# A streaming encoder step on one core: the first block's loads re-timed, the forget chain cut in three, one scaling moved to ScalarE

## The chip, the core and the metric

The kernel runs on one core of a Trainium2 chip. TensorE (PE in the profile) multiplies matrices; PEld is its loading of the stationary operand. VectorE (DVE), ScalarE (ACT) and GpSimd (POOL) do elementwise work. SyncE (SP) issues nearly all DMAs. Each engine works through its own instructions in order, and waits on semaphores for the others and for DMAs. The metric is the device time of one execution, in microseconds (us).

## The reference

One layer of a hybrid encoder takes 2048 prompt frames and 64 sample frames that have a cache of 512 earlier ones. All is float32 with D = 1024.

```python
h = rmsnorm(x, g_pre)
fq, fk, fv, ff, fg, dq, dk, dv, dg = split(h @ w_in)          # widths 512, ff 8
logf = log_sigmoid(ff + b_f);  cum = cumsum(logf)             # over cache and new frames
# fox: 8 heads of 64, causal
s = fq.fk / 8 + cum[q] - cum[k];  fox_o = softmax(s) @ fv
# diff: 4 heads, two halves of 64, chunk-causal, T5 bias by relative position
lam = exp(sum(lq1*lk1)) - exp(sum(lq2*lk2)) + 0.2
p = softmax(q1.k1/8 + bias) - lam * softmax(q2.k2/8 + bias);  diff_o = p @ dv
diff_o = rmsnorm(diff_o, subln_g) * 0.8
mixed = concat(fox_o * silu(fg), diff_o * silu(dg))
y = x + rmsnorm(mixed @ w_out, g_post)
```

The results are y for prompt and sample, and the new rows of fk, fv, logf, dk and dv.

## The kernel before

Matrices are multiplied in split form: each operand is a rounded part (h) and a remainder (l), and three products hh, hl, lh are summed in PSUM. So each weight tile that is loaded is cast on ScalarE (`wh`, L776) and subtracted on VectorE or GpSimd (`wl`, L777).

**Blocks.** The prompt is cut into four blocks of 512 frames (tiles of 128 frames; the sample is a fifth tile, number 16, of block 0). `Proj.block(b)` projects one block, group by group: in blocks 0 and 2 the order is fv, fg, fk, fq, dg, dk, dq, dv, in blocks 1 and 3 the reverse. A group takes eight weight tiles of 128x512, one for each 128 rows. `nat` makes one frame tile of a natural group (8 steps of three matmuls, then an evacuation `nat_out` that scales by the row's 1/rms, `rs`); `qgroup` makes q transposed. The loop counts groups with `gi`. Block 0 is different: its weights go through staging tiles `wst` in the pool "pp" (8 tiles, two weight tiles in each), its first group (`nat_first`) multiplies all five frame tiles step by step into five PSUM buffers, and the first two tiles of its second group use the PSUM tag "pt" (three buffers), which they share with `ptq`, the sums of squares of x that VectorE reads into `xv` (L1123), and with the forget logits' accumulators. In its first four groups block 0 rotates its accumulators over five PSUM buffers (`acc`).

**Side work.** `stats(b+1)` squares the next block's x: loads `xn` (L1072), squares with a sum on ScalarE (L1084), then a short column step and a row step. Its pieces are appended one by one after frame tiles of groups 2 to 5. `forget(b)` makes the eight forget logits, and returns functions that come later: `columns` (log-sigmoid on small tiles, L1163 to L1188, on ScalarE and VectorE in turn), `sums` (cumulative sum to DRAM, `CUM`) and in block 0 `sample` (the same for the cache: loads `crev` (L1212), scans it (L1216), writes `csum`). `prologue2` loads subln, the lambda vectors `lamt` (L1415), relT and cbias, computes lambda, and builds the line of relative biases on GpSimd.

**Attention.** `Attn` runs about one block behind, interleaved with the next projection. It asks for keys (`kg`, pool "kk"), values, q, biases (`bias` and `strip`, pool "bb", two tiles) and gates (pool "gg", two tiles) ahead of use, in rings. `diff` makes the scores of both halves; exponentials `prob` are up to 2048 keys wide in two tiles of 1024. `combine` scales the second softmax by a per-row factor `cc` and adds it to the first: for keys up to 1024 in one VectorE instruction (L596), beyond that by a scaling (L593) and an addition (L594), both on GpSimd. `Out` multiplies by w_out beside the last block's attention and at the end.

**Order.** Every piece of work is a function with an estimated cost. They are put on one list, `line`, with a place in time in estimated TensorE microseconds; `put` spreads a list over an interval, and single entries have a fixed place (prologue 20, prologue2 110). The list is sorted and called, and the framework's list scheduler then orders each engine's instructions, moving work ahead when, by its own estimate, its inputs and a buffer of its pool are there. A pool with n buffers under a tag makes the n+1st tile wait until the first one is released. The pool "ef" has four tiles of 128x512, tag "er" two.

Of the kernel before, what the change touches and what calls it, by code (L numbers as in the profile page):

```python
# [91 lines left out]
def hybrid_step(ctx: ExitStack, tc: tile.TileContext, ins, outs):  # L92
# [68 lines left out]
    class Attn:  # L161
# [393 lines left out]
        def diff(self, u, pair, ctxu, last, sample=False):  # L555
# [9 lines left out]
            for j, t in enumerate(tiles):  # L565
# [14 lines left out]
                def combine(j=j, n=n):  # L580
                    if j == 0:
                        e["c"] = sm.tile([P, 2], F32, name="ci", tag="ci")
                    st = sts[j]
                    c = sm.tile([P, 2], F32, name="cc", tag="cc")
                    st[0]["total"]()
                    st[1]["total"]()
                    nc.vector.reciprocal(out=c[:rows, 0:1], in_=st[1]["s"][:rows, 0:1])
                    nc.vector.scalar_tensor_tensor(out=c[:rows, 1:2], in0=st[0]["s"][:rows, 0:1], scalar=neglam[:rows],
                                                   in1=c[:rows, 0:1], op0=ALU.mult, op1=ALU.mult)
                    for h, c0 in enumerate(range(0, n, 2 * BLK)):  # L590
                        p0, p1 = (x["P"][h][:rows, :min(n - c0, 2 * BLK)] for x in st)
                        if h:
                            nc.gpsimd.tensor_scalar(out=p1, in0=p1, scalar1=c[:rows, 1:2], scalar2=None, op0=ALU.mult)  # L593
                            nc.gpsimd.tensor_tensor(out=p0, in0=p0, in1=p1, op=ALU.add)  # L594
                        else:
                            nc.vector.scalar_tensor_tensor(out=p0, in0=p1, scalar=c[:rows, 1:2], in1=p0, op0=ALU.mult,  # L596
                                                           op1=ALU.add)
                    nc.vector.reciprocal(out=e["c"][:rows, j:j + 1], in_=st[0]["s"][:rows, 0:1])
# [124 lines left out]
    class Proj:  # L723
# [72 lines left out]
        def block(self, b):  # L796
# [27 lines left out]
            for gi, g in enumerate(order):  # L824
# [10 lines left out]
                else:  # L835
# [3 lines left out]
                    for tt in ts:  # L839
                        last = tt[-1] == tl[-1]  # L840
                        th += self.nat(b, g, tt, w, x, cols, st, last and ends, last and lastg)
                        if 2 <= gi <= 5:
                            th += sq[:1]
                            sq = sq[1:]
                        if b == 0 and gi == 1 and tt[0] == tl[2]:
                            th += row0
                        if gi == 1 and tt[0] == tl[0]:
                            th += [(0.1, fn) for fn in after[:1]]
                            after = after[1:]
                        elif gi == 1 and tt[0] == tl[1 if b else 2]:  # L850
                            th += [(0.1, fn) for fn in after]
                            after = []
                if b and gi == 0:
# [153 lines left out]
        def qgroup(self, b, g, w, x, nt, st, freew):  # L1007
# [4 lines left out]
            for c in range(4):  # L1012
                e = {}
                for i, segs in enumerate(pieces):
# [22 lines left out]
                    def evac(c=c, i=i, e=e, segs=segs, t0=t0, N=N):  # L1037
                        f = self.p["e"].tile([P, BLK], F32, name="qf", tag="ef")
                        hl = self.p["raw"].tile([P, BLK], F32R, name="qhl", tag="raw") if nt > BLK and not i else \
                            self.p["e"].tile([P, 2 * BLK], F32R, name="qhl", tag="er", bufs=2)  # L1040
                        nc.vector.tensor_tensor(out=f[:, :N], in0=e[i][:, :N], in1=st["rbc"][:, t0:t0 + N],
# [15 lines left out]
        def stats(self, b, st):  # L1057
# [4 lines left out]

            todo = [(i, t, hf) for i, t in enumerate(tl) for hf in (0, 1)]


            lead = 2 if b == 1 else 1

            def load(n):
                i, t, hf = todo[n]
                e[n] = self.p["raw"].tile([P, BLK], F32, name="xn", tag="raw") if b == 1 else \  # L1070
                    self.p["e"].tile([P, BLK], F32, name="xn", tag="ef")
                nc.sync.dma_start(out=e[n], in_=xp[t * P:(t + 1) * P, hf * BLK:(hf + 1) * BLK])  # L1072

            def square(n):
                def go():
                    i, t, hf = todo[n]
                    if not n:
                        e["ss"] = sm.tile([P, 2, 8], F32, name="xss", tag="xss", bufs=2)
                        nc.vector.memset(e["ss"], 1.0)
                        for m in range(lead):  # L1080
                            load(m)
# [47 lines left out]
        def forget(self, b, x, nt, st):  # L1129
# [5 lines left out]
            def alloc():  # L1135
                e["z"] = self.p["raw"].tile([P, BLK + DEC], F32, name="z8", tag="z", bufs=1)
            th.append((0.0, alloc))
            for c0, N in ((0, BLK), (BLK, DEC))[:1 + (b == 0)]:
# [17 lines left out]
            def columns():  # L1156
# [19 lines left out]
                nc.scalar.activation(out=a, in_=a, func=AF.Exp, scale=-1.0)  # L1176
                d, lw, m = e["fd"], e["fl"], e["fm"]
                nc.vector.tensor_scalar(out=d, in0=a, scalar1=1.0, scalar2=None, op0=ALU.add)
                nc.scalar.activation(out=lw, in_=d, func=AF.Ln)
                nc.vector.tensor_scalar(out=d, in0=d, scalar1=-1.0, scalar2=None, op0=ALU.add)  # L1180
# [22 lines left out]
            def sample():  # L1203
# [4 lines left out]
                nc.tensor.transpose(pt[:8, :DEC], z[:DEC, 32:40], ident[:DEC, :DEC])  # L1208
                c = self.p["e"].tile([P, BLK], F32, name="csum", tag="ef")[:8]
                c2 = sm.tile([8, DEC], F32, name="csn", tag="csn", bufs=1)  # L1210
                r = self.p["e"].tile([P, BLK], F32, name="crev", tag="ef")[:8]
                nc.sync.dma_start(out=r, in_=clf)  # L1212
                nc.vector.tensor_tensor_scan(out=c2, data0=ones[:8].to_broadcast([8, DEC]), data1=pt[:8, :DEC],
# [188 lines left out]
    def prologue(e):  # L1402
# [6 lines left out]
        nc.sync.dma_start(out=fb, in_=bass.AP(fbias.tensor, fbias.offset, [[0, P], [1, 8]]))  # L1409

    def prologue2(e):
        nc.sync.dma_start(out=subl, in_=subln)

        lam = e.tile([P, BLK], F32, name="lamt", tag="ef")
        nc.sync.dma_start(out=lam[:, :256], in_=bcast_row(lams, 256))  # L1415
        ee = sm.tile([P, 4], F32, name="lame", tag="lame", bufs=1)
        for i in (0, 1):
            nc.vector.tensor_tensor_reduce(out=lam[:, 256:320], in0=lam[:, 128 * i:128 * i + 64],
                                           in1=lam[:, 128 * i + 64:128 * i + 128], scale=1.0, scalar=0.0,
# [4 lines left out]

        rt = sm.tile([4, 32], F32, name="relT", tag="relT", bufs=1)
        nc.sync.dma_start(out=rt, in_=relT)
        nc.sync.dma_start(out=cbias, in_=bass.AP(relT.tensor, relT.offset + 15, [[0, P], [32, 4]]))
        nc.vector.tensor_scalar(out=cbias, in0=cbias, scalar1=-1.0, scalar2=None, op0=ALU.mult)
# [134 lines left out]
```

## Time and profile before

| | us |
|---|---|
| median of 3 runs | 1772.97 (1772.33 to 1780.28) |
| profiled execution | 1778.38 |
| its span in the profile | 1776.6 |
| TensorE busy | 1715.1 (97%) |
| weight loads busy | 1462.7 (82%) |
| VectorE busy | 1208.8 (68%) |
| ScalarE busy | 1127.0 (63%) |
| GpSimd busy | 761.7 (43%) |

The span is the time between the first and the last recorded instruction. A row of waits reads: who waited, for whom, total us, how often, the longest. A row of a timeline reads: start, length, engine, line, operation, output<-inputs, shape, count, and in square brackets how long the engine was idle before it and what ended that. A row of a window gives each engine's busy time and instruction count, the granted TensorE clock (1.00 is full speed), the mean busy share of the 16 DMA engines and GB/s.

### The profile page before, as it was taken

The numbers are of one execution on the slowest core, as the hardware profiler recorded it, in microseconds if no ns is written. First come the engines' busy times: TensorE is split into PE (matmuls) and PEld (weight loads), VectorE is DVE, ScalarE is ACT, GpSimd is POOL, SyncE is SP. The second block draws the span as 40 slices with busy tenths as digits, with TensorE's granted clock in tenths as the row PEclk, the third lists the DMA queues.
The fourth block names the chain that finished last, engine by engine and source line by source line (L and its number), as shares of the span: only waits on it lengthen the run. The fifth ranks groups of instructions, "written<-read, shape, count | busy, mean of one in ns | idle before, by whom it ended". The sixth has DMA issues, their size and how long they took to land.

```text
span 1776.6 us, 31312 instructions
## 1 busy us (share of the span) xinstructions
PE 1715.1 (97%) x9844; PEld 1462.7 (82%) x9844; DVE 1208.8 (68%) x3289; ACT 1127.0 (63%) x2518; POOL 761.7 (43%) x1075
## 2 busy tenths in 40 slices
PE   8899999999999999999999999999989999999998
PEld 6697988888787877888888888888878888888887
DVE  5424565566786666766777687877788787767674
ACT  5636465586676765675676567667676656666663
POOL 2313135364444533443324235645685655323341
PEclk9899999999999999999999999999999999999999
DMA  9785688889767667877677666767674455355433
GB/s 249 229 218 185 201 279 284 242 268 278 210 224 242 209 184 222 260 206 243 213 249 212 208 178 196 225 201 224 204 235 155 158 184 180 129 204 166 155 109 111
DMA packets 278981, 369.94 MB, mean 208 GB/s; under 512 B 32080, under 2 KB 167404, under 8 KB 278816
## 3 DMA queue, kind: packets, MB, share of 16 engines
q1 hardware_dynamic: 278000, 365.57, 67.0%
q0 software_dynamic: 672, 2.38, 0.5%
q8 instruction: 78, 1.28, 0.3%
q14 instruction: 87, 0.71, 0.1%
q10 hardware_dynamic: 144, 0.00, 0.0%
HBM read 263.87 MB, written 106.35 MB: 208 GB/s over the span
## 4 chain that ended last, share of the span: by engine, by line
PE 71%; DMA 11%; DVE 6%; ACT 4%; issue 3%; POOL 3%; SPq 1%; DVEq 0%; POOLq 0%; ACTq 0%
PE S L348 11%; PE pt L487 8%; PE acc L871 8%; PE acc L872 7%; PE acc L873 7%; PE av L518 6%; PE avd L518 4%; PE acc L1026 3%; PE acc L1027 3%; PE acc L1028 3%; DMA wraw<-in_w_in 3%; PE acco L1325 2%; PE acco L1327 2%; PE acco L1326 2%; ACT prob L369 2%
## 5 line engine op out<-in xcount | busy, mean ns | idle before, releaser
L369 ACT ACTIVATE prob<-prob,mn 128x1024 f32<-128x1024 f32 (+8 forms) x400 | 356.6, 893 | 152.8 <-DVE mn L356 151.6
L348 PE MATMUL S<-kg,qg 128*128 128x512 f32 (+4 forms) x1344 | 370.7, 371 | 10.9 <-DVE mn L356 6.1
L494 DVE TENSOR_TENSOR ptl<-pt,pth 128x512 fp32r<-128x512 f32 (+3 forms) x456 | 283.6, 637 | 80.1 <-ACT pth L493 77.7
L871 PE MATMUL acc<-wh,xx 128*128 128x512 f32 x752 | 300.6, 403 | 14.3 <-DVE xv L1123 6.2
L872 PE MATMUL acc<-wl,xx 128*128 128x512 f32 x752 | 299.5, 400 | 3.9 <-DVE wl L777 3.9
L873 PE MATMUL acc<-wh,xx 128*128 128x512 f32 x752 | 298.6, 398 | 0.3 <-DVE xx L745 0.2
L493 ACT CAST pth<-pt 128x512 fp32r<-128x512 f32 (+3 forms) x456 | 238.1, 546 | 91.1 <-PE pt L487 78.4
L487 PE MATMUL pt<-ident,prob 128*128 128x128 f32 (+2 forms) x1692 | 256.4, 273 | 7.7 <-DVE prob L596 5.2
L348 PEld LDWEIGHTS S<-kg,qg 128*128 128x128 f32 (+1 forms) x1344 | 225.5, 187 | 46.4 <-DVE mn L356 11.5
L487 PEld LDWEIGHTS pt<-ident,prob 128*128 128x128 f32 (+2 forms) x1692 | 199.3, 141 | 28.1 <-DVE prob L596 6.1
L777 POOL TENSOR_TENSOR wl<-wraw,wh 128x512 fp32r<-128x512 f32 x126 | 169.7, 1363 | 90.9 <-ACT wh L776 85.0
L871 PEld LDWEIGHTS acc<-wh,xx 128*128 128x128 f32 x752 | 143.4, 191 | 43.8 <-issue 6.6
L872 PEld LDWEIGHTS acc<-wl,xx 128*128 128x128 f32 x752 | 143.4, 191 | 30.0 <-DVE wl L777 4.6
L873 PEld LDWEIGHTS acc<-wh,xx 128*128 128x128 f32 x752 | 143.0, 190 | 28.6 <-DVE xx L745 1.2
L518 PE MATMUL av<-pth,vg 128*128 128x256 f32 (+1 forms) x576 | 157.5, 292 | 3.9 <-ACT pth L493 2.3
L405 POOL TENSOR_TENSOR dg<-bias,cmask 128x128 f32<-128x128 f32 (+1 forms) x136 | 65.2, 479 | 208.6 <-DVE mn L356 134.0
L450 POOL TENSOR_SCALAR gate<-gate,rr 128x64 f32<-128x64 f32 (+1 forms) x136 | 64.2, 482 | 182.8 <-DMA gate<-GS 98.9
L518 PE MATMUL av<-ptl,vg 128*64 128x256 f32 (+1 forms) x576 | 138.2, 281 | 1.5 <-DVE ptl L494 1.5
L776 ACT CAST wh<-wraw 128x512 fp32r<-128x512 f32 x168 | 100.6, 621 | 58.3 <-DMA wraw<-in_w_in 44.1
L518 PE MATMUL avd<-pth,vg 128*128 128x256 f32 (+1 forms) x576 | 131.4, 287 | 0.4 <-ACT pth L493 0.4
L356 DVE CUSTOM_DVE_ANT_0 prob<-S,bias,mn 128x512 f32<-128x512 f32 (+4 forms) x200 | 115.4, 577 | 13.6 <-PE S L348 6.6
L518 PEld LDWEIGHTS av<-pth,vg 128*128 128x128 f32 x576 | 109.5, 191 | 14.2 <-ACT pth L493 2.7
(261 smaller groups left out, 3604.6 us busy)
## 6 DMA issues: line engine op xcount, KB each, us to landing
wraw<-in_w_in SPq DMA_DIRECT2D x168, 256.0 KB, 5.2
vg<-VS SPq DMA_DIRECT2D x80, 512.0 KB, 6.3
qg<-QD SPq DMA_DIRECT2D x128, 256.0 KB, 4.4
kg<-KS SPq DMA_DIRECT2D x64, 512.0 KB, 5.1
wst<-in_w_in SPq DMA_DIRECT2D x64, 256.0 KB, 6.3
out<-ef SPq DMA_DIRECT2D x64, 256.0 KB, 2.6
VS<-vhl SPq DMA_DIRECT2D x32, 512.0 KB, 4.8
KS<-khl SPq DMA_DIRECT2D x32, 512.0 KB, 4.4
```

The lines of the kernel that those rows point to most:

```text
L348: nc.tensor.matmul(S[:rows, :c1 - c0], q()[s][:, qc:qc + rows], kg()[ki][:, c0 - k0:c1 - k0], start=(s == 0), stop=(s == 1))
L356: nc.vector.tensor_tensor_reduce(out=pr[:rows, a - p0:b - p0], in0=S[:rows, a - c0:b - c0], in1=ap()[:rows, a - b0:b - b0], scale=1.0, sca ...
L369: nc.scalar.activation(out=pr, in_=pr, func=AF.Exp, scale=-1.0, bias=st["m"][:rows, i - 1:i], accum_out=st["s"][:rows, h:h + 1])
L487: nc.tensor.transpose(pt[:rk, off:off + rows], self.key_tile(sts[j], rows, kt, rk), ident[:rows, :rows])
L493: nc.scalar.copy(h[:rk, :off], pt[:rk, :off])
L494: nc.vector.tensor_tensor(out=l[:rk, :off], in0=pt[:rk, :off], in1=r32(h[:rk, :off]), op=ALU.subtract)
L518: nc.tensor.matmul(st["av"][:vs.stop - vs.start, j0 * rows:W], ctxu["v"][kt // 4][:rk, kt % 4, vs], g["p"][part][:rk, o:o + w], start=(kt ...
L776: nc.scalar.copy(h, raw[:, :BLK])
L777: (nc.vector if many or k % 4 == 3 else nc.gpsimd).tensor_tensor(out=l, in0=raw[:, :BLK], in1=r32(h), op=ALU.subtract)
L871: nc.tensor.matmul(a, x[0][:, c0:c0 + rows], wh, start=s, stop=False)
L872: nc.tensor.matmul(a, x[0][:, c0:c0 + rows], wl, start=False, stop=False)
L873: nc.tensor.matmul(a, x[1][:, c0:c0 + rows], wh, start=False, stop=e)
```

## The change

Six edits:

1. `stats`: the pieces are appended in block 0 after tiles of groups 4 and 5 only, and block 1's x is loaded as four tiles of 128x1024 in pool "pp" (before: eight of 128x512 in pool "raw").
2. `sample`: `crev` and `csum` share one tile of pool "bb" (before: two "ef" tiles), and the load of crev stands at the start of `forget`.
3. `loads2`, new, at place 60: the four loads of `prologue2`, with the lambda vectors in a tile of the gate pool (before: an "ef" tile, at place 110).
4. `qgroup`: in block 0 the second q tile of fq comes from the key pool (before: tag "er").
5. `forget`: `columns` is cut into three functions, appended after one frame tile of group 1 each; in block 0 the sums and the sample follow a tile later.
6. `combine`: the scaling beyond 1024 keys is a ScalarE activation.

```diff
                         if h:
-                            nc.gpsimd.tensor_scalar(out=p1, in0=p1, scalar1=c[:rows, 1:2], scalar2=None, op0=ALU.mult)
+                            nc.scalar.activation(out=p1, in_=p1, func=AF.Copy, scale=c[:rows, 1:2])
                             nc.gpsimd.tensor_tensor(out=p0, in0=p0, in1=p1, op=ALU.add)
...
-                        if 2 <= gi <= 5:
+                        if (2 if b else 4) <= gi <= 5:
                             th += sq[:1]
                             sq = sq[1:]
...
                         if gi == 1 and tt[0] == tl[0]:
                             th += [(0.1, fn) for fn in after[:1]]
                             after = after[1:]
-                        elif gi == 1 and tt[0] == tl[1 if b else 2]:
-                            th += [(0.1, fn) for fn in after]
-                            after = []
+                        elif gi == 1 and (b or tt[0] != tl[1]):
+                            n = 1 if b or tt[0] == tl[2] else len(after)
+                            th += [(0.1, fn) for fn in after[:n]]
+                            after = after[n:]
...
                         hl = self.p["raw"].tile([P, BLK], F32R, name="qhl", tag="raw") if nt > BLK and not i else \
+                            self.p["k"].tile([P, 2 * BLK], F32R, name="qhl", tag="k") if nt > BLK and g == "fq" else \
                             self.p["e"].tile([P, 2 * BLK], F32R, name="qhl", tag="er", bufs=2)
...
-            todo = [(i, t, hf) for i, t in enumerate(tl) for hf in (0, 1)]
-            lead = 2 if b == 1 else 1
+            parts, w = (1, D) if b == 1 else (2, BLK)
+            todo = [(i, t, hf) for i, t in enumerate(tl) for hf in range(parts)]
+            lead = 1
             def load(n):
                 i, t, hf = todo[n]
-                e[n] = self.p["raw"].tile([P, BLK], F32, name="xn", tag="raw") if b == 1 else \
+                e[n] = self.p["p"].tile([P, 2 * BLK], F32, name="xn", tag="p") if b == 1 else \
                     self.p["e"].tile([P, BLK], F32, name="xn", tag="ef")
-                nc.sync.dma_start(out=e[n], in_=xp[t * P:(t + 1) * P, hf * BLK:(hf + 1) * BLK])
+                nc.sync.dma_start(out=e[n], in_=xp[t * P:(t + 1) * P, hf * w:(hf + 1) * w])
...
             def alloc():
                 e["z"] = self.p["raw"].tile([P, BLK + DEC], F32, name="z8", tag="z", bufs=1)
+                if b == 0:
+                    t = self.p["b"].tile([P, BW], F32, name="crev", tag="b")
+                    e["rev"], e["csum"] = t[:8, :BLK], t[:8, BLK:]
+                    nc.sync.dma_start(out=e["rev"], in_=clf)
...
-            return th, [columns, sums] + ([sample] if b == 0 else [])
+            return th, [columns, columns2, columns3, sums] + ([sample] if b == 0 else [])
...
+    def loads2(g):
+        nc.sync.dma_start(out=subl, in_=subln)
+        held["lam"] = g.tile([P, 2, P], F32, name="lamt", tag="g").rearrange("p a c -> p (a c)")
+        nc.sync.dma_start(out=held["lam"], in_=bcast_row(lams, 256))
+        held["rt"] = sm.tile([4, 32], F32, name="relT", tag="relT", bufs=1)
+        nc.sync.dma_start(out=held["rt"], in_=relT)
+        nc.sync.dma_start(out=cbias, in_=bass.AP(relT.tensor, relT.offset + 15, [[0, P], [32, 4]]))
...
             line.append((20.0, len(line), lambda: prologue(pe)))
+            line.append((60.0, len(line), lambda: loads2(pools["g"])))
             line.append((110.0, len(line), lambda: prologue2(pe)))
```

The first of the three parts of `columns` ends after the two activations (Abs, Exp), the second is the addition of 1 and the Ln (L1178, L1179), the third the nine small VectorE instructions and the store.

More of the change, by code (lines that the diff above doesn't have):

```diff
@@ L1079, in go @@
                         nc.vector.memset(e["ss"], 1.0)
+                        if parts == 1:
+                            nc.vector.memset(e["ss"][:, 1, :], 0.0)
                         for m in range(lead):
@@ L1176, in columns, with columns2, columns3 @@
                 nc.scalar.activation(out=a, in_=a, func=AF.Exp, scale=-1.0)
-                d, lw, m = e["fd"], e["fl"], e["fm"]
-                nc.vector.tensor_scalar(out=d, in0=a, scalar1=1.0, scalar2=None, op0=ALU.add)
-                nc.scalar.activation(out=lw, in_=d, func=AF.Ln)
+            def columns2():
+                nc.vector.tensor_scalar(out=e["fd"], in0=e["fa"], scalar1=1.0, scalar2=None, op0=ALU.add)
+                nc.scalar.activation(out=e["fl"], in_=e["fd"], func=AF.Ln)
+            def columns3():
+                z, a, d, lw, m = (e[nm] for nm in ("fz", "fa", "fd", "fl", "fm"))
                 nc.vector.tensor_scalar(out=d, in0=d, scalar1=-1.0, scalar2=None, op0=ALU.add)
@@ L1208, in sample @@
                 nc.tensor.transpose(pt[:8, :DEC], z[:DEC, 32:40], ident[:DEC, :DEC])
-                c = self.p["e"].tile([P, BLK], F32, name="csum", tag="ef")[:8]
+                c, r = e["csum"], e["rev"]
                 c2 = sm.tile([8, DEC], F32, name="csn", tag="csn", bufs=1)
-                r = self.p["e"].tile([P, BLK], F32, name="crev", tag="ef")[:8]
-                nc.sync.dma_start(out=r, in_=clf)
                 nc.vector.tensor_tensor_scan(out=c2, data0=ones[:8].to_broadcast([8, DEC]), data1=pt[:8, :DEC],
@@ L1409, in prologue @@
         nc.sync.dma_start(out=fb, in_=bass.AP(fbias.tensor, fbias.offset, [[0, P], [1, 8]]))
+    held = {}
+    def loads2(g):
[5 more added lines that the diff above has]
+        nc.sync.dma_start(out=cbias, in_=bass.AP(relT.tensor, relT.offset + 15, [[0, P], [32, 4]]))
     def prologue2(e):
-        nc.sync.dma_start(out=subl, in_=subln)
-        lam = e.tile([P, BLK], F32, name="lamt", tag="ef")
-        nc.sync.dma_start(out=lam[:, :256], in_=bcast_row(lams, 256))
+        lam, rt = held["lam"], held["rt"]
         ee = sm.tile([P, 4], F32, name="lame", tag="lame", bufs=1)
         for i in (0, 1):
-            nc.vector.tensor_tensor_reduce(out=lam[:, 256:320], in0=lam[:, 128 * i:128 * i + 64],
+            nc.vector.tensor_tensor_reduce(out=lam[:, 128 * i:128 * i + 64], in0=lam[:, 128 * i:128 * i + 64],
                                            in1=lam[:, 128 * i + 64:128 * i + 128], scale=1.0, scalar=0.0,
@@ L1423, in prologue2 @@
         nc.vector.tensor_scalar(out=neglam, in0=neglam, scalar1=LAM_INIT, scalar2=None, op0=ALU.subtract)
-        rt = sm.tile([4, 32], F32, name="relT", tag="relT", bufs=1)
-        nc.sync.dma_start(out=rt, in_=relT)
-        nc.sync.dma_start(out=cbias, in_=bass.AP(relT.tensor, relT.offset + 15, [[0, P], [32, 4]]))
         nc.vector.tensor_scalar(out=cbias, in0=cbias, scalar1=-1.0, scalar2=None, op0=ALU.mult)
```

## The prediction

> **What bounds the kernel now.** I read the page first: busy shares, slices, the chain. Then the chip time by stretches, TensorE's waits, and the timelines of the engines it waited for.
>
> ```profile
> span 1776.6 us, 31312 instructions
> PE 1715.1 (97%) x9844; PEld 1462.7 (82%) x9844; DVE 1208.8 (68%) x3289; ACT 1127.0 (63%) x2518; POOL 761.7 (43%) x1075
> PE   8899999999999999999999999999989999999998
> PEclk9899999999999999999999999999999999999999
> PE 71%; DMA 11%; DVE 6%; ACT 4%; issue 3%; POOL 3%; SPq 1%; DVEq 0%; POOLq 0%; ACTq 0%
> ```
>
> TensorE is busy 97% of the span, so all idle time together is 1776.6 − 1715.1 = 61.5 us. The thin slices are the first two and the last, and the granted clock dips in the second. A change that touches no matmul can win only idle time and slow clock. Where they lie, by stretches (TensorE busy first, then weight loads, DVE, ACT, POOL, granted clock, DMA share):
>
> ```profile
> 0.00:45.00 45.00, 36.26 (x170) 27.96 (x170) 25.29 (x41) 23.72 (x43) 12.25 (x15) 0.99 0.90 247
> 45.00:82.00 37.00, 32.08 (x132) 25.23 (x133) 14.37 (x37) 23.02 (x50) 11.27 (x14) 0.92 0.69 231
> 82.00:124.00 42.00, 42.00 (x236) 37.02 (x235) 14.42 (x25) 17.70 (x32) 7.24 (x4) 0.96 0.89 205
> 124.00:150.00 26.00, 22.79 (x126) 20.10 (x125) 11.59 (x34) 9.65 (x26) 14.38 (x45) 0.93 0.91 282
> 150.00:350.00 200.00, 199.28 (x1099) 169.33 (x1098) 106.94 (x313) 113.87 (x263) 68.84 (x101) 1.00 0.75 232
> 1040.00:1480.00 440.00, 427.11 (x2453) 368.20 (x2452) 352.09 (x896) 298.09 (x662) 263.69 (x287) 0.99 0.62 193
> ```
>
> From 0 to 150 us, where block 0 is projected, 16.9 us are idle (8.7 + 4.9 + 0 + 3.2). The next 200 us lose 0.7. TensorE's waits in the first 150 us:
>
> ```profile
> PE acc L871 <- DVE xv L1123: 6.2, 1, 6.2
> PE acc L872 <- DVE wl L777: 3.9, 1, 3.9
> PE acc L871 <- ACT wh L776: 3.7, 2, 3.2
> PE acc L871 <- ACT xx L744: 0.9, 1, 0.9
> PE ptf L1195 <- DVE fz L1187: 0.6, 1, 0.6
> ```
>
> Three single stops (6.2, 3.9, 3.2) carry it. After each, TensorE runs slowly for a while (matmuls in a stretch, granted clock):
>
> ```profile
> 45.40:50.60 5.20, 5.17 (x12) 0.50 0.78 256
> 80.50:85.10 4.60, 4.56 (x13) 0.63 0.68 247
> 138.30:143.10 4.80, 4.72 (x13) 0.64 0.97 319
> ```
>
> The time lost is length × (1 − clock): 2.6 + 1.7 + 1.7 = 6.0 us. The waits name vector and scalar instructions that were only victims. What stood ahead of them is in the timelines of DVE, ACT and SP (start, length, instruction, idle before it and who ended that):
>
> ```profile
> 45.08 0.21 DVE L1123 TENSOR_SCALAR xv<-ptq 128x4 f32<-128x4 f32 x2
> 48.92 0.17 DVE L1428 TENSOR_SCALAR cbias<-cbias 128x4 f32<-128x4 f32 x1 [2.75 <-DMA cbias<-in_relT]
> 78.22 1.21 DVE L1216 TENSOR_TENSOR_SCAN crev<-ones,crev 8x512 f32<-8x512 f32 x1 [7.13 <-DMA crev<-in_clf]
> 136.28 0.22 DVE L1418 CUSTOM_DVE_ANT_0 lamt<-lamt 128x64 f32<-128x64 f32 x1 [6.91 <-DMA lamt<-in_lams]
> 40.24 0.63 ACT L1084 ACTIVATE xn<-xn 128x512 f32<-128x512 f32 x1 [7.72 <-DMA xn<-in_xp]
> 78.85 0.69 ACT L881 ACTIVATE ef<-acc,xrs 128x512 f32<-128x512 f32 x1 [5.08 <-DMA GS<-ef]
> 124.42 0.55 ACT L1049 CAST qhl<-qf 128x256 fp32r<-128x256 f32 x2 [7.55 <-DMA KS<-khl]
> 136.81 0.20 ACT L1421 ACTIVATE lame<-lame 128x2 f32<-128x2 f32 x1 [7.90 <-DVE lame L1418]
> 29.82 6.69 SPq L1072 DMA_DIRECT2D xn<-in_xp  x5
> 131.86 1.61 SPq L1415 DMA_DIRECT2D lamt<-in_lams  x1
> ```
>
> **The change part by part.** *Block 1's loads of x held back (xn).* They were issued from 29.82; ScalarE, in order, sat 7.72 us at the first square. Behind it were the casts wh of the next weights, behind those DVE's wl, behind those xv, whose PSUM buffer TensorE needed. With xn in the pool of the weight staging tiles and squared only in groups 4 and 5, nothing of this stands there: 6.2 + 2.6 = 8.8 us go. Next late there would be the gate group's first weights, whose casts no longer wait; I count no rest.
>
> *crev and csum out of the evacuation pool, crev loaded at the start of the forget chain.* DVE's 7.13 us wait goes, and with two more of the four "ef" buffers free so should ScalarE's 5.08 us wait for an output (GS<-ef). Both stood ahead of the weight pairs: 3.9 + 1.7 = 5.6 us go.
>
> *lam, relT, cbias, subln asked for at 60 instead of 110, lam in the gate pool.* lam was issued only at 131.86, when an "ef" buffer came free; DVE then waited 6.91 us for it, ScalarE 7.90, and behind ScalarE were the casts of the next group: 3.2 + 1.7 = 4.9 us go. The four DMAs now stand ahead of weight loads on SP's queue, at no more than lam's 1.61 us of issue each, 6.4 us in all. The waits above hold no TensorE stop on a late weight load after the first few microseconds, so the queue has that much room and I count 0 (upper end 6.4). The cbias wait (2.75 us, ahead of the scale for the first evacuation) goes too, with no TensorE stop of its own.
>
> These three make −19.3 us. [...]
>
> *What is given back in block 0.* Squares: four of 128x1024 instead of eight of 128x512. Rows near them:
>
> ```profile
> L1084 ACT ACTIVATE xn<-xn 128x512 f32<-128x512 f32 x24 | 15.1, 628 | 24.7 <-DMA xn<-in_xp 24.6
> L369 ACT ACTIVATE prob<-prob,mn 128x1024 f32<-128x1024 f32 x160 | 184.1, 1152 | 100.4 <-DVE mn L356 99.6
> L369 ACT ACTIVATE prob<-prob,mn 128x128 f32<-128x128 f32 x32 | 12.7, 396 | 6.5 <-DVE mn L356 6.4
> L348 PE MATMUL S<-kg,qg x76: 220/329/477, 188.4 to 338.4; 128*128 128x128 f32 x20, 128*128 128x256 f32 x20, 128*128 128x384 f32 x20, 128*128 128x512 f32 x16
> ```
>
> That is 4 × 1.15 = 4.6 us for 8 × 0.63 = 5.0. ScalarE will still wait for xn, at a new place: the staging tiles come free as fq's weights are cast, so xn is loaded while fq is multiplied. In that group ScalarE already sat 7.55 us (124.42) and TensorE did not stop, for block 0 rotates five accumulators. So 0; the upper end is a stop like the third, 4.9 us, if the wait falls on the casts at a handover. dk's weights then queue behind xn's 2 MB for a staging tile, with the whole dg group as cover; if that is too short, rival (a) is what follows.
>
> fq's second q tile moves into the k pool's four tiles and makes the first key loads wait; keys are first multiplied at 188.4, so 0. crev takes one of two bias tiles and lam one gate tile: also first needed by attention there, 0. The forget sums come one tile later, against the same 188.4: 0.
>
> Denser DMA: from 45 to 150 the DMA engines were busy 25.5 + 37.4 + 23.7 = 86.6 us; in 19.3 us less that would be full, unless late work slides into the 150 to 350 stretch at 0.75. The first stretch, at 0.90, lost 0.9 us in 45 to late x; over 86 us that is 1.7, I take 2 us (ends 0 and 8).
>
> *Forget chain in three parts (blocks 1 to 3; in 1 and 3 group 1 is a q group, which takes no pieces, and the parts follow it in a row).* One stop seems to belong to it:
>
> ```profile
> 638.76 0.98 PE L348 MATMUL S<-kg,qg 128*128 128x384 f32 x2 [2.35 <-DVE fd L1178]
> 637.32 1.02 DVE L777 TENSOR_TENSOR wl<-wraw,wh 128x512 fp32r<-128x512 f32 x1 [1.71 <-ACT wh L776]
> 636.67 0.62 ACT L776 CAST wh<-wraw 128x512 fp32r<-128x512 f32 x1 [2.48 <-DMA wraw<-in_w_in]
> ```
>
> But read upwards from the last row it is a late weight load that held ScalarE, DVE and then TensorE; fd was merely last to finish. Splitting removes none of that: 0, with ends −2.4 and +0.6 (the ptf wait).
>
> *Second softmax scaled on ScalarE.* The two GpSimd rows, and TensorE's longest waits between 1040 and 1480 us:
>
> ```profile
> L593 POOL TENSOR_SCALAR prob<-prob,cc x32: 900/2528/3937, 1055.2 to 1464.6; 128x128 f32<-128x128 f32 x4, 128x256 f32<-128x256 f32 x4, 128x384 f32<-128x384 f32 x4, 128x512 f32<-128x512 f32 x4
> L594 POOL TENSOR_TENSOR prob<-prob x32: 451/1514/2794, 1056.9 to 1469.1; 128x128 f32<-128x128 f32 x4, 128x256 f32<-128x256 f32 x4, 128x384 f32<-128x384 f32 x4, 128x512 f32<-128x512 f32 x4
> PE pt L487 <- DVE prob L596: 4.6, 2, 3.1
> PE acc L871 <- ACT ef L881: 2.2, 2, 1.3
> ```
>
> 32 instructions of median 2.5 us, some 80 us, leave GpSimd. No long wait of TensorE names GpSimd, so the shorter path by itself gains 0. ScalarE gains 32 × (1.15 + 0.40)/2 = 25 us: 298 of 440 becomes 323, its idle time 142 becomes 117. Waits on it like the 2.2 us would grow by about a fifth, and each new instruction waits in order for DVE's factor cc: I take +1 us. Ends: −4.6, if the prob stops go, and +16, if every one holds ScalarE, and through it TensorE, half a microsecond. [...]
>
> Sum: −19.3 + 2 + 1 = −16.3 us. The profiled execution took 1778.4 (span 1776.6, 1.8 around it), 5.4 above the median 1773.0. From the median the sum gives 1756.7, from the profiled execution 1762.1; should part of those 5.4 us be longer stops of the same kind, the truth lies between. I take 1758.
>
> **The rivals.** (a) One stop is replaced: the held-back xn, or a weight load behind it, holds ScalarE at a handover. For it: ScalarE stood 5 to 8 us for a DMA, or for something held by one, four times in this part, and the DMA share nears 1. Against: five accumulators. It returns 4.9 to 8.8 us: 1763 to 1767.
>
> (b) The stops move and don't go: a transfer that is asked for earlier still lands late in a full DMA system, and the list order after it shifts. Half to all of 19.3 comes back, 1768 to 1775. For it: the three causes were all waits of about 7 us for a DMA, far more than the lists they stand in allowed for. Against: each is now asked for a whole group or more ahead of its use.
>
> (c) Slower: ScalarE's 32 new instructions each stand waiting for cc, and the exponentials and the copies of the transposed softmax behind them come late. In its 142 us of idle time there is room, but not if it is spent blocked. It cancels the gain at 16.3 / 32 = 0.5 us of stop each, beyond the +1 counted, and makes the kernel slower by 0.5% (8.9 us) at 0.8 us each; 1 us each gives 1758 + 32 = 1790. Against: TensorE's stops on ScalarE's evacuations there are 2.2 us in 440.
>
> [...]
>
> **How the numbers follow.** Forecast 0.45, (d) 0.10, (a) 0.18, (b) 0.17, (c) 0.10. 0.5% is 8.9 us, about what a measurement of this kernel tells from no change, so faster means below 1764.1. Faster: the forecast, (d) and three fifths of (a): 0.66. Slower: 0.08 of (c). Same: 0.26. The range runs from 1749 (everything won, the fd and prob stops too) to 1772, which leaves out a third of (b) and all of (c).
>
> **What would show it.** In the new profile TensorE's waits before 150 us hold no xv, wl or wh stop over 2 us, and the clock's second slice is whole; ScalarE squares xn in 128x1024 well after 90 us; DVE waits under 2 us for crev and lamt; all that follows sits some 16 us earlier. The forget part is wrong if the 638 us stop goes though wraw is still late. The ScalarE part is wrong if TensorE's waits on ScalarE between 1040 and 1480 grow by more than 3 us. The prediction fails if a new stop over 3 us stands before 150 us, or if the later stretches, which lose some 44 us (61.5 − 16.9 − 0.7), lose 10 more.

## The result and the profile after

The kernel after takes 1766.73 us (median of 20 runs, 1756.94 to 1771.43). The kernel before, run beside it on the same chips, takes 1776.81 us (20 runs, 1772.33 to 1783.7). The ratio is 0.9937, with a 95% interval of 0.9925 to 0.9948, so the change wins 9 to 13 us. The time lies in the predicted range, and 8.7 us above the predicted 1758. It is not below 1764.1, the prediction's line for faster; against the kernel before that ran beside it, it is 0.57% less, a little past the 0.5% that this line stood for. The profiled execution of after took 1761.82 us against 1778.38 before.

The page of after, its first lines, slices and chain:

```profile
span 1760.0 us, 31267 instructions
PE 1712.5 (97%) x9844; PEld 1459.2 (83%) x9844; DVE 1186.6 (67%) x3290; ACT 1142.3 (65%) x2542; POOL 693.2 (39%) x1043
PE   8999999999999999999999999999999999999998
PEclk9999999999999999999999999999999999999999
PE 67%; DMA 13%; ACT 6%; issue 5%; DVE 5%; POOL 2%; SPq 1%; DVEq 0%; ACTq 0%; POOLq 0%
```

The second slice of the clock no longer dips. TensorE's idle time is 1760.0 − 1712.5 = 47.5 us, 14.0 less than before. About 7 of the 14 lie in the first 200 us, and 5.8 where the forecast had none, from 400 to 800 us. The windows of before and of after (TensorE busy first):

```profile
400.00:800.00 400.00, 385.82 (x2196) 321.77 (x2195) 279.29 (x795) 271.41 (x633) 183.25 (x299) 0.99 0.75 226
```

```profile
400.00:800.00 400.00, 391.64 (x2270) 327.89 (x2269) 274.63 (x808) 277.12 (x640) 186.42 (x298) 1.00 0.76 230
```

TensorE's waits in the first 200 us are these (engine, tile and line, releaser: total, times, longest):

```profile
PE acc L872 <- ACT wh L776: 3.9, 2, 3.4
PE acc L872 <- DVE xv L1127: 3.7, 1, 3.7
PE idle L1408 <- DVE xss L1081: 1.3, 1, 1.3
PE ptq L1122 <- POOL xsq L755: 0.7, 1, 0.7
PE av L518 <- ACT pth L493: 0.3, 1, 0.3
```

Two of the three old stops are gone (wl near 80 us, wh near 138 us). The first, the xv stop, is still there with 3.7 of its 6.2 us, and there is a new one. The timeline gives their places, and the windows behind them the slow clock (matmuls in a stretch, granted clock, DMA share):

```profile
43.75 0.47 PE L872 MATMUL acc<-wh,xx 128*128 128x512 f32 x1 [3.68 <-DVE xv L1127]
154.81 1.22 PE L872 MATMUL acc<-wh,xx 128*128 128x512 f32 x2 [3.39 <-ACT wh L776]
```

```profile
0.00:200.00 200.00, 190.07 (x969) 160.40 (x970) 91.38 (x201) 109.42 (x213) 57.98 (x94) 0.97 0.79 227
43.70:48.00 4.30, 4.25 (x12) 3.37 (x13) 0.68 (x4) 3.42 (x9) 0.28 (x1) 0.60 0.89 302
154.80:160.00 5.20, 5.19 (x12) 4.09 (x13) 5.18 (x7) 5.20 (x11) 1.59 (x1) 0.50 0.02 8
100.00:140.00 40.00, 40.00 (x258) 37.36 (x258) 18.61 (x42) 20.56 (x45) 16.73 (x46) 1.00 1.03 297
```

The three old stops cost 13.3 us and 6.0 us of slow clock. The two of after cost 3.7 + 3.4 us, and 4.3 × 0.40 + 5.2 × 0.50 = 4.3 us of slow clock, together 11.4. So some 8 us net were won here, where the forecast had 19.3 less 2. The last row shows the DMA engines full from 100 to 140 us.

What stands ahead of each stop is in the timelines of the other engines:

```profile
31.86 1.36 SPq L1427 DMA_DIRECT2D lamt<-in_lams  x1
33.64 0.59 SPq L1430 DMA_DIRECT2D cbias<-in_relT  x1
38.93 0.23 DVE L1437 CUSTOM_DVE_ANT_0 lamt<-lamt 128x64 f32<-128x64 f32 x1 [5.81 <-DMA lamt<-in_lams]
41.80 0.17 DVE L1444 TENSOR_SCALAR cbias<-cbias 128x4 f32<-128x4 f32 x1 [2.49 <-DMA cbias<-in_relT]
42.18 1.29 DVE L777 TENSOR_TENSOR wl<-wst,wh 128x512 fp32r<-128x512 f32 x2
43.39 0.21 DVE L1127 TENSOR_SCALAR xv<-ptq 128x4 f32<-128x4 f32 x2
138.89 1.29 POOL L1003 TENSOR_TENSOR ef<-ef,gw 128x512 f32<-128x512 f32 x1 [5.67 <-ACT gw L1002]
149.69 1.32 SPq L1005 DMA_DIRECT2D GS<-ef  x2
152.96 0.63 ACT L998 ACTIVATE gw<-ef 128x512 f32<-128x512 f32 x1 [8.48 <-DMA GS<-ef]
```

First stop: the small loads, asked for ahead, were used ahead as well. VectorE stands first for lamt and then for cbias, which lands about 8 us after its issue, and only then makes the two weight residuals and xv, on which TensorE waits. The wait that before stood on ScalarE (for xn) now stands on VectorE (for lamt and cbias).

New stop: GpSimd finished the gate output at 140.2 us, but SyncE issued its store at 149.69. ScalarE stood 8.48 us for that buffer, with the weight casts of the next group behind it. What held SyncE's queue between 126 and 152 us:

```profile
SPq L1054 <- DMA wst<-in_w_in: 5.5, 3, 2.2
SPq L194 <- DMA QN<-qhl: 3.8, 1, 3.8
SPq L773 <- DMA wst<-in_w_in: 2.2, 1, 2.2
```

The second row is a key load that waits for the tile of the key pool which now holds a q tile. The other rows are stores of q and a load that wait for weight loads to land. The stores of q have no data in common with a weight load. Counted in SyncE's timeline, the weight load that each of these four DMAs waits for is the one issued eight before it. So in these 7.7 us (5.5 + 2.2) late landings of weight loads held all that stood behind them on the queue.

Beyond 1024 keys (1024 to 1464 us) TensorE's longest waits are now on ScalarE:

```profile
PE acco L1335 <- ACT z L1351: 3.9, 4, 1.5
PE S L348 <- DVE mn L356: 2.9, 7, 1.2
PE pt L487 <- ACT pts L634: 2.2, 1, 2.2
```

The prob stops (4.6 us) are gone, and these came or grew: before, z was 0.7 us and mn 2.0 us.

### The profile page after: what moved, and what is told of

Same layout as the page of the kernel before. It is cut to its first block, busy times and chain, and to the rows that moved or that the text cites. A ratio compares the mean times of both kernels' runs of the same rounds, so it can differ in the third digit from the quotient of the medians.

```text
span 1760.0 us, 31267 instructions
## 1 busy us (share of the span) xinstructions
PE 1712.5 (97%) x9844; PEld 1459.2 (83%) x9844; DVE 1186.6 (67%) x3290; ACT 1142.3 (65%) x2542; POOL 693.2 (39%) x1043
## 3 DMA queue, kind: packets, MB, share of 16 engines
q8 instruction: 78, 1.28, 0.3%
## 4 chain that ended last, share of the span: by engine, by line
PE 67%; DMA 13%; ACT 6%; issue 5%; DVE 5%; POOL 2%; SPq 1%; DVEq 0%; ACTq 0%; POOLq 0%
PE S L348 10%; PE pt L487 7%; PE acc L872 7%; PE acc L873 7%; PE acc L874 7%; PE av L518 5%; PE avd L518 4%; DMA wraw<-in_w_in 3%; PE acco L1335 3%; PE acco L1336 3%; PE acco L1337 3%; PE acc L1027 3%; PE acc L1028 3%; PE acc L1029 3%; DMA wst<-in_w_in 2%
## 5 line engine op out<-in xcount | busy, mean ns | idle before, releaser
L348 PE MATMUL S<-kg,qg 128*128 128x512 f32 (+4 forms) x1344 | 373.9, 371 | 10.2 <-DVE mn L356 6.6
L872 PE MATMUL acc<-wh,xx 128*128 128x512 f32 x752 | 300.0, 402 | 10.8 <-ACT wh L776 5.5
L356 DVE CUSTOM_DVE_ANT_0 prob<-S,bias,mn 128x512 f32<-128x512 f32 (+4 forms) x200 | 115.3, 576 | 15.3 <-DMA bias<-CUM 5.6
```

Source lines behind the costliest of these rows:

```text
L348: nc.tensor.matmul(S[:rows, :c1 - c0], q()[s][:, qc:qc + rows], kg()[ki][:, c0 - k0:c1 - k0], start=(s == 0), stop=(s == 1))
L356: nc.vector.tensor_tensor_reduce(out=pr[:rows, a - p0:b - p0], in0=S[:rows, a - c0:b - c0], in1=ap()[:rows, a - b0:b - b0], scale=1.0, sca ...
L872: nc.tensor.matmul(a, x[0][:, c0:c0 + rows], wh, start=s, stop=False)
```

## The experiments

Theory: the gain is the removal of TensorE's stops in the first block, and the rest of the forecast was kept back there by two new waits, one on VectorE (small loads used early) and one behind SyncE's queue. Rivals: the ScalarE scaling took it back; the loads' gains add up and other edits cost; the transfers as such are the limit. All kernels ran beside the kernel before, whose medians were 1779.33, 1777.88, 1776.89 and 1778.24 us in the four groups (c, d, e, f). "Idle" below is TensorE's idle time in the first 200 us of a profile, 200 less the busy time of that stretch: 16.9 before, 9.9 after. Times in us against before are worked out from the ratios.

**First group: the kernel after, with one part undone each.**

`c0_after` is the kernel after, unchanged.

> The changed kernel once more, as the base for the three kernels beside it on the same chip: 0.994 of the kernel before (its 20 runs gave 0.9937), and in the profile again two TensorE stops in block 0: xv near 43.8 us (3.7 us) and wh near 154.8 us (3.4 us). If those stops are accidents of one execution, they are absent or elsewhere here.

1763.53 us, ratio 0.9919 (0.9896 to 0.9942). Its profile has the same xv stop (4.04 us) and the same wh stop at 156.5 us (3.37 us), so both belong to the program and not to one execution.

`c1_no_kpool` leaves the q tile out of the key pool:

```
-  self.p["k"].tile([P, 2 * BLK], F32R, name="qhl", tag="k") if nt > BLK and g == "fq" else \
```

> The changed kernel with the second q tile of fq back under tag er, as before. Theory: the q tile in the key pool made the first key load wait on SP for its release (3.8 us), the outputs GS queued behind it were issued 9 us late, ScalarE waited 8.5 us for an output buffer and TensorE 3.4 us; without it the stop at 154.8 goes with its 2.6 us of slow clock, so 4 to 6 us less than the changed kernel. Rival: the stop comes from the 16 DMA engines being full between 100 and 140 us (share above 1.0), so SP waits for older DMAs whatever the tile: then the stop stays, and the time is within 1 us of the changed kernel.

1760.83 us, ratio 0.9899 (0.9878 to 0.9919). No key load waits on SyncE's queue now; the gate store goes out at 145.63 us and the new stop shrinks:

```profile
152.10 0.73 PE L872 MATMUL acc<-wh,xx 128*128 128x512 f32 x2 [1.87 <-ACT wh L776]
```

The xv stop is down to 0.6 us as well, which this edit doesn't touch: here cbias landed before VectorE had done with lamt (cbias used at 39.30 us, not 41.80), and TensorE came to this point about 1 us later, its clock being 0.86 from 30 to 38 us (1.00 in after). The direction is that of the theory, but the stop only halved and the intervals of c0 and c1 overlap. Without the key load the store was still issued some 6.6 us after GpSimd had finished (138.98 us).

`c2_loads_early` asks for the small loads at 5 in the order of work:

```
-  line.append((60.0, len(line), lambda: loads2(pools["g"])))
+  line.append((5.0, len(line), lambda: loads2(pools["g"])))
```

> The changed kernel with the four small loads (lam, relT, cbias, subln) at place 5 instead of 60. Theory: they were issued at 30 to 34 us and landed at 38.9 and 41.8, while VectorE had their users ahead of the weight pairs and xv; asked for 20 us earlier they have landed, the 3.7 us stop at 43.8 goes with about 1.7 us of slow clock: 4 to 5.5 us less. Rival: they delay the first x and weight loads instead, TensorE stops by 1 to 3 us in the first 33 us and the net is 0 to -3 us.

1763.64 us, ratio 0.992 (0.99 to 0.994), no better than c0. The xv stop is gone, as the theory says, but a stop of 1.90 us came at 66.8 us, and the one at 153 us stayed at 3.55: idle 9.0 us.

`c3_gpsimd_scale` puts the second softmax's scaling back on GpSimd:

```
-  nc.scalar.activation(out=p1, in_=p1, func=AF.Copy, scale=c[:rows, 1:2])
+  nc.gpsimd.tensor_scalar(out=p1, in0=p1, scalar1=c[:rows, 1:2], scalar2=None, op0=ALU.mult)
```

> The changed kernel with the scaling beyond 1024 keys back on GpSimd. Theory (gain in block 0 alone): within 2 us of the changed kernel; TensorE idle between the forget chain of block 3 and the tail as before. Rival 1: ScalarE's 25 us are paid in part, then this is 2 to 5 us faster than the changed kernel. [...]

1761.08 us, ratio 0.99 (0.9878 to 0.9922). The prob stops are back (1.45 and 2.99 us) and the kernel is no slower. The scaling carries none of the gain.

**Second group: the kernel before, with one edit of the change each.**

`d1_xn_held`: the second block's x loads held back, in tiles of the staging pool and squares of 128x1024:

```
-  if 2 <= gi <= 5:
+  if (2 if b else 4) <= gi <= 5:
...
-  e[n] = self.p["raw"].tile([P, BLK], F32, name="xn", tag="raw") if b == 1 else \
+  e[n] = self.p["p"].tile([P, 2 * BLK], F32, name="xn", tag="p") if b == 1 else \
```

> The kernel before, with the hold-back of the second block's xn loads and their squares in four wide pieces, and nothing else of the change. Theory 'stops add up': the stop of 6.2 us at 39 us is caused by ScalarE waiting for xn while the weight casts stand behind it, so it goes, and 2.6 us of slow clock with it; the stops at 80 and at 138 us stay: -8.8 us, ratio 0.995, time 1770. No new stop at 155 us, since VectorE meets no early lamt here. Rival 'full transfers': the transfers stay full either way, and the stops at 80 and 138 us, or one at 155 us, grow by what the first one loses: -3 us or less, ratio 0.998 to 1.0.

1763.48 us, ratio 0.9939 (0.9918 to 0.9961): −10.8 us, about as much as the whole change in its 20 runs. And not for the reason expected. Its stops and what VectorE and ScalarE waited for:

```profile
42.45 0.47 PE L871 MATMUL acc<-wh,xx 128*128 128x512 f32 x1 [2.94 <-DVE xv L1124]
72.78 1.19 PE L871 MATMUL acc<-wh,xx 128*128 128x512 f32 x4 [2.67 <-ACT wh L776]
40.78 0.17 DVE L1429 TENSOR_SCALAR cbias<-cbias 128x4 f32<-128x4 f32 x1 [6.39 <-DMA cbias<-in_relT]
69.58 0.06 DVE L1219 MEMSET csum<- 8x1 f32 x1 [4.91 <-DMA RS<-rrow]
70.93 1.21 DVE L1217 TENSOR_TENSOR_SCAN crev<-ones,crev 8x512 f32<-8x512 f32 x1 [1.28 <-issue]
71.53 0.69 ACT L881 ACTIVATE ef<-acc,xrs 128x512 f32<-128x512 f32 x1 [6.19 <-DMA GS<-ef]
130.83 0.25 DVE L1419 CUSTOM_DVE_ANT_0 lamt<-lamt 128x64 f32<-128x64 f32 x1 [2.41 <-DMA lamt<-in_lams]
```

The first stop is not gone but halved, and on cbias. That load keeps its place in the order of work, but with no xn loads ahead of it on SyncE it went out at 35.02 us (42.26 before), and VectorE's use of it now stands ahead of xv (before: behind it). The stop at 80 us is now 2.67, and the one at 138 us is gone. Ahead of crev's scan VectorE stood 4.91 + 1.28 = 6.19 us in a row, little less than the 7.13 before, and ScalarE stood 6.19 us for a gate store (5.08 before) with the casts behind it. lamt was used 4.1 us after its issue (126.75 to 130.83), before 4.4 us (131.86 to 136.28): it didn't land faster. It was issued 5 us earlier, and VectorE made six weight residuals between 124 and 128.4 us, ahead of it, where before it made none from 124.9 us until it had lamt.

`d2_crev_early`: crev and csum in a tile of their own, crev loaded ahead:

```
+  if b == 0:
+      t = self.p["b"].tile([P, BW], F32, name="crev", tag="b")
+      e["rev"], e["csum"] = t[:8, :BLK], t[:8, BLK:]
+      nc.sync.dma_start(out=e["rev"], in_=clf)
```

> The kernel before, with crev and csum loaded ahead into a tile of their own, and nothing else. Theory 'stops add up': the stop of 3.9 us near 80 us goes with its 1.7 us of slow clock: -5.6 us, ratio 0.997. Rival 'full transfers': what is gained at 80 us comes back in the stop at 138 us or a new one at 155 us: within 2 us of before.

1770.37 us, ratio 0.9967 (0.9951 to 0.9982): −5.9 us. The stop at 80 us is gone. The next one moved to 133.5 us and is longer than its 3.2 us before, so a part came back:

```profile
133.50 1.22 PE L871 MATMUL acc<-wh,xx 128*128 128x512 f32 x2 [4.93 <-ACT wh L776]
```

`d3_loads_early`: lamt, relT, cbias and subln asked for ahead:

```
+  line.append((60.0, len(line), lambda: loads2(pools["g"])))
   line.append((110.0, len(line), lambda: prologue2(pe)))
```

> The kernel before, with lamt, relT, cbias and subln asked for ahead as in the kernel after, and nothing else. The stop near 138 us (3.2 us and 1.7 of slow clock) goes. But lamt and cbias now join full transfers beside the xn loads, and VectorE waits for them ahead of the weight residuals (5.8 and 2.5 us in the kernel after): the theory that early small loads cost expects the stop at 39 us to grow from 6.2 us by 1 to 4 us, so between -4 and +1 us in all. The prediction's own account expects -4.9 us and the first stop unchanged.

1770.01 us, ratio 0.9956 (0.994 to 0.9973): −7.8 us, more than either account gave. The first stop is 6.5 us, with VectorE standing 4.37 us for lamt and 2.03 for cbias ahead of it; the stop at 138 us is gone, and of the one at 80 us, which this edit wasn't thought to touch, 1.5 us are left, although VectorE still stood 6.8 us for crev.

`d4_scalar_scale`: the scaling moved to ScalarE:

```
-  nc.gpsimd.tensor_scalar(out=p1, in0=p1, scalar1=c[:rows, 1:2], scalar2=None, op0=ALU.mult)
+  nc.scalar.activation(out=p1, in_=p1, func=AF.Copy, scale=c[:rows, 1:2])
```

> The kernel before, with the second softmax's scaling moved from GpSimd to ScalarE and nothing else. TensorE's stops for prob (1.45 and 3.1 us) go, and stops behind ScalarE's z and pts come in their place: within 3 us of before either way, and no part of the 11 us. Rival: this edit carries part of the gain, 4.6 us of stops: -4 us or more.

1775.87 us, ratio 0.9991 (0.9974 to 1.0009): nothing. TensorE's waits between 1040 and 1480 us, from its profile:

```profile
PE S L348 <- DVE mn L356: 5.5, 8, 2.8
PE acco L1325 <- ACT z L1341: 3.4, 3, 1.4
PE avd L518 <- DVE ptl L494: 2.0, 1, 2.0
```

The prob stops went, and others took their place. In this stretch GpSimd was busy for 196.5 us (263.7 before) and VectorE for 346.6 (352.1 before), but TensorE gained nothing: its idle time there is 13.0 us, and was 12.9.

**Third group: do the loads add up, and where is the new stop made?**

`e1_three_loads`: the edits of d1, d2 and d3 together, nothing else.

> The kernel before with the three load edits together (xn held back, crev and csum ahead, lamt/relT/cbias/subln ahead), without the q tile in the key pool, the forget chain in parts and the ScalarE scaling. Alone these gave -10.8, -5.9 and -7.8 us against the median of before. Theory 'one shared cause' (each of them relieves the same transfers, so they replace one another): -10 to -15 us, with 7 to 10 us of TensorE idle in the first 200 us. Rival 'they add up': -20 us or more, idle under 3 us; the kernel after would then owe its smaller gain to the other edits.

1764.38 us, ratio 0.992 (0.9901 to 0.9939): −14.2 us, with idle at 5.1 us and no stop of 1.4 us or more in that stretch. The three alone sum to −24.5 us (±5.5, from their intervals), together they give −14.2 (±3.4): they replace one another. That this is so is shown; that full transfers are the one cause is not, for the same sum comes out when each edit moves the order of work at several stops, as d1 and d3 did. Nor is the early use of lamt and cbias gone. VectorE waits for them here as in after, and TensorE only comes to that point 2.2 us later, mostly because it ran slowly ahead of it (a clock of 0.80 from 38 to 45 us, 0.95 in after):

```profile
41.31 0.17 DVE L1437 TENSOR_SCALAR cbias<-cbias 128x4 f32<-128x4 f32 x1 [2.21 <-DMA cbias<-in_relT]
38.00:45.00 7.00, 5.98 (x35) 3.36 (x33) 2.82 (x15) 2.22 (x6) 0.00 (x0) 0.80 0.84 256
```

So a part of the lost time has the form of slow clock and not of a stop. This kernel, with neither the q tile in the key pool nor the split chain, has no stop near 150 us.

`e2_gate_on_gpsimd_queue`: the kernel after, with all stores of the first block's gate output (ten, in two groups) issued from GpSimd.

```
-  nc.sync.dma_start(out=GN[:, c0:c0 + BLK] if t == 16 else
+  q = nc.gpsimd if b == 0 else nc.sync
+  q.dma_start(out=GN[:, c0:c0 + BLK] if t == 16 else
```

> The kernel after, with the first block's gate output (GS<-ef) issued from GpSimd, which computes it, and not from SyncE. Theory 'SyncE's queue makes the stop at 154.8 us' (the store was ready at 140.2 us and issued at 149.7): the store goes out by 142 us, ScalarE finds its buffer free, the stop of 3.4 us and its 2.6 us of slow clock go: -4 to -6 us against the kernel after (ratio to before near 0.990). Rival 'the transfers themselves are the limit': the store goes out early but ScalarE's casts then wait for the weight rows (wst), and the stop stays within 1 us: 0 to -1 us.

1757.99 us, ratio 0.9888 (0.9868 to 0.9909), clear of the 0.9925 to 0.9948 of after in its 20 runs, though not of c0's 0.9896 to 0.9942. From its timeline:

```profile
138.16 1.29 POOL L1003 TENSOR_TENSOR ef<-ef,gw 128x512 f32<-128x512 f32 x1 [8.04 <-ACT gw L1002]
139.74 0.62 POOL L1006 DMA_DIRECT2D GS<-ef  x1 [0.30 <-POOL ef L1003]
145.69 0.63 ACT L998 ACTIVATE gw<-ef 128x512 f32<-128x512 f32 x1 [1.94 <-DMA GS<-ef]
```

and TensorE's waits in the first 200 us:

```profile
PE acc L872 <- DVE xv L1128: 2.9, 1, 2.9
PE idle L1409 <- DVE xss L1082: 1.3, 1, 1.3
PE acc L872 <- ACT xx L744: 1.0, 2, 0.8
PE acc L872 <- ACT wh L776: 0.5, 1, 0.5
```

The store goes out 0.3 us after it is ready, ScalarE stands 1.94 us and not 8.48, and the new stop is gone. The transfer itself is no faster: ScalarE goes on 6.0 us after the issue, against 3.3 us in after. The DMA share from 100 to 140 us is still 1.03, and a key load still waits 4.0 us on SyncE. So SyncE's order made that stop, and full transfers alone did not.

`e3_both_mends`: the edits of c1 and c2 together.

> The kernel after without the first q tile in the key pool, and with the small loads asked for at 5 in the order of work and not at 60. Each mend alone left 6.6 and 8.9 us of TensorE idle in the first 200 us (9.9 in the kernel after). Theory: the stop at 43.8 us goes with the earlier loads, the one near 153 us shrinks to under 2 us: idle of 4 to 6 us there, ratio to before 0.988 to 0.990, time 1758. Rival: the stop at 67 us that the earlier loads brought (1.9 us) and the one at 152 us stay, no better than either mend alone (0.990 to 0.992).

1760.69 us, ratio 0.9912 (0.9892 to 0.9931). Both stops are gone and 1.42 us at 66.8 us are left, idle 6.1 us; by time it is not to be told from c1 or c2, so the expected 0.988 to 0.990 was missed.

**Last run.** `f1_all_mends`: the kernel after with the edits of c1, c2, c3 and e2.

> The kernel after with all mends: no q tile in the key pool, small loads asked for at 5, the first block's gate output issued from GpSimd, and the second softmax scaled on GpSimd again. Theory 'what each mend removes stays removed': idle of 4 to 5 us in the first 200 us, 13 us instead of 15.8 us between 1200 and 1600 us, and a ratio to before of 0.986 to 0.988, time 1753 to 1756. Rival 'the mends replace one another, as the loads did': no better than the gate store from GpSimd alone, 0.988 to 0.991.

1752.65 us (5 runs, 1750.03 to 1754.78), ratio 0.9849 (0.9825 to 0.9872): about 27 us under the kernel before, the best kernel here, and a little past its expected range. Its page and its two long stops:

```profile
span 1750.9 us, 31320 instructions
PE 1706.3 (97%) x9844; PEld 1457.1 (83%) x9844; DVE 1197.4 (68%) x3290; ACT 1125.2 (64%) x2510; POOL 767.9 (44%) x1085
```

```profile
67.37 1.20 PE L872 MATMUL acc<-wh,xx 128*128 128x512 f32 x4 [2.94 <-ACT wh L776]
1297.04 0.87 PE L487 MATMUL pt<-ident,prob 128*128 128x128 f32 x6 [3.29 <-DVE prob L596]
```

Idle in the first 200 us is 5.3, against 6.6 in e2. All idle time together is 1750.9 − 1706.3 = 44.6 us, no less than e2's 43.3 (1756.7 − 1713.4). The rest of the difference is TensorE's busy time, 7.1 us less at a clock of 0.995 against 0.993. Why there is less slow clock, and which of the four edits it is owed to, was not settled.

**What no run tried alone: the split forget chain.** It is the only part that sets two groups of profiles apart: eight profiles have it (after, c0 to c3, e2, e3, f1), six don't (before, d1 to d4, e1), and each other part is either in e1 too or left out of one of the eight. TensorE's idle time between 400 and 800 us is 6.5 to 10.2 us in the eight (mean 8.6) and 11.0 to 14.2 in the six (mean 12.7). The groups don't overlap. So some 4 us hang on the split, or on the order of work that it shifts; as no kernel has it alone, that is inferred and not shown.

## Why the prediction was right, and where it was not

**The total: right, in part by luck; its composition: not.** Against its own profile the forecast was −16.3 us and the profile after shows −16.6. That match is luck: by the medians the change is −10.1, and the profiled execution of after is the fourth fastest of 20. In the profile the first block gave some 8 us and not 17, and the stretch from 400 to 800 us, forecast at 0, gave 5.8 us of idle time. A stop of 2.35 us with slow clock behind it, at 638 us in the profile of before, also is absent from that of after; c0, the same kernel, has a stop of 3.72 us in that place, so this part is chance. Of the signs that the prediction named, the xv stop over 2 us and VectorE's 5.81 us for lamt spoke against it; the whole second slice of the clock and the late wide squares came as said, and the new stop, idle from 151.4 us on, lies just beyond its 150 us.

**"xn held back: 8.8 us; I count no rest": wrong in where it acts.** Alone it gave 10.8 us, yet not by removing the first stop, of which 2.9 us stayed (cbias). In its trace what stands behind it on SyncE and ScalarE comes earlier and VectorE's order is another, and with that the second stop is shorter and the third is gone. It did not clear xn's transfers out of the way of crev and lamt: in before seven of the eight xn loads were issued by 46.4 us and squared by 55, the eighth was issued at 139.92, and crev and lamt were issued at 70.91 and 131.86. The step that failed is reading each stop as owned by the one load ahead of it, so that the three could be summed. At the second stop d3 shows this too: VectorE's wait for crev stayed at 6.8 us and the stop fell from 3.87 to 1.50. ScalarE's wait for the gate store stood there as well (5.08 us before, 6.19 in d1, 4.18 in d3), and in d2, where it is gone, the stop is gone. Why the gains replace one another is open beyond that.

**"crev 5.6" and "lam 4.9": near as edits alone (−5.9 ± 2.8, −7.8 ± 2.9), wrong as terms of a sum.** On top of the first, the two add 3.4 us (e1 against d1, with overlapping intervals). Lam's number is in part luck, since d3 also took 2.4 us off the stop at 80 us. That lamt waited for an "ef" buffer the trace doesn't show: it names TensorE's acc (L1028) for the 1.6 us ahead of that issue.

**"The cbias wait goes too, with no TensorE stop of its own": wrong.** The early loads were used early, and their 8 us of landing put VectorE's wait ahead of xv: 3.7 us and 1.7 of slow clock. The price of 0 to 6.4 us for these four was sought in SyncE's time of issue; it lay in VectorE's order of work.

**"fq's second q tile … keys are first multiplied at 188.4, so 0": wrong.** It named the data's user and not the queue behind the waiting load. On SyncE the gate store stood behind it and behind other waits, and its cost was a stop of 3.4 us and 2.6 of slow clock at 154.8 us. Moving the gate stores (e2) gave 8.7 us against after's 20 runs, and 5.5 us, within the noise, against c0. The tile is one part of it: without it the stop was 1.9 us, and in e1, without the split chain too, there was none. Whether the rest belongs to the split was not tried.

**"Denser DMA: 2 us (ends 0 and 8)": mis-sized.** The share did rise to 1.03. The first stop, which stands behind late landings, cost 5.4 us with its slow clock, inside the ends. The 6.0 us of the new one came from SyncE's order, for which the sum has no term.

**Squares, 0: right.** Four of 128x1024 took 1.06 us each from 104.8 us on, and TensorE didn't stop there.

**Forget chain, 0 (ends −2.4 and +0.6): probably mis-sized.** Its reading of the stop at 638 us is mostly borne out: where the chain is split, a stop on a late weight row stays near 620 us (1.64 us in after), and the fd stop, else 0.7 us or less, came back once (2.33 us in c3). But it looked at that stop alone. The stops that are missing with the split are others: waits for VectorE's mn (L356), which sum to 2.2 to 4.0 us between 400 and 800 us in the six profiles without it, are not among the seven longest of any of the eight.

**ScalarE scaling, +1: right within what can be measured** (−1.6 ± 3.1 alone). By the forecast's own test it failed: TensorE's waits on ScalarE rose from 3.9 us to 10.4 between 1040 and 1480 us, and to 8.3 in the same work, which lies 16 us earlier. But they took the place of the prob stops: all idle time in this work is 12.4 us, and was 12.9.

**The rivals.** The time, 1766.7, lies at the upper end of (a)'s 1763 to 1767, and (a) has the form of the new stop: ScalarE held at a handover with the casts behind it. Its cause was not (a)'s, though, neither xn nor a late weight load, but a store stuck in SyncE's queue. (b) said that a transfer asked for earlier still lands late and that the order after it shifts, with half or more of 19.3 us coming back. That is what lamt and cbias did at the first stop, and 11.4 of the 19.3 us are there again; with the gain after 400 us the time stayed a little below (b)'s 1768. ((b)'s upper end should have been 1758 + 19.3 = 1777 and not 1775.) For (d), 0.10 in the chances, no run shows a ground: with the scaling off GpSimd and nothing else changed (d4), the time moved by −1.6 ± 3.1 us.

## What to carry to other kernels

When several waits for different DMAs stand close together on the same in-order queues, don't add up their prices: relieving one can move the order at the next. Here three edits were worth 24.5 us alone and 14.2 together. Do the cheapest one and look again. A load asked for earlier can be used earlier as well: here cbias, issued at 33.64 us and not at 42.26, was used at 41.80 and not at 48.92, and VectorE's 2.49 us for it stood ahead of xv. So check what stands behind the first use on its in-order engine. And when a tile changes its pool, follow the waiting DMA on its issuing queue: here a gate store that was ready at 140.2 us went out at 149.69, behind a key load that waited 3.8 us for such a tile, and ScalarE stood 8.48 us for the store's buffer. Issued from GpSimd, which makes the data, the store went out 0.3 us after it was ready, and ScalarE stood 1.94 us.

## What was not expected of the hardware

A short stop can be followed by as much slow clock as a long one: 2.5 us of it came after a stop of 1.58 us in e2, 2.6 after one of 3.39 in after and 2.6 after one of 6.2 in before. From e2, right behind a stop of 1.58 us at 611.11 us:

```profile
611.00:616.00 5.00, 4.89 (x20) 4.36 (x21) 3.20 (x13) 3.97 (x10) 4.53 (x5) 0.51 0.83 247
```

and from after, right behind one of 1.64 us at the same place of the work:

```profile
618.00:626.00 8.00, 7.16 (x42) 5.24 (x42) 4.89 (x19) 6.30 (x18) 6.73 (x8) 1.00 0.89 261
```

The first cost 2.5 us of clock, the second none, so between these two the length of the stop doesn't decide. What does was not shown. Such dips come and go between executions: two profiles of the same kernel after have spans of 1760.0 and 1769.9 us, at clocks of 0.995 and 0.989. So a single pair of profiles of this kernel can't tell a change of less than some 10 us.
